# A hybrid decoder block on one core: the causal 31-tap convolution as three half-length filters on even and odd tokens

## The chip, the core and the metric

The kernel runs on one core of a Trainium2 chip. Its engines work at the same time, each on its own queue in order: TensorE (PE, with its weight loads PEld), VectorE (DVE), ScalarE (ACT), GpSimd (POOL) and SyncE (SP), which issues the transfers. The metric is the device time of one execution in microseconds, the median of several runs.

## The reference

2048 tokens of width 1024, in float32. A normalised input is projected by one matrix `w_in` into all sections; a convolution branch and an attention branch are gated, projected and merged.

```python
h = rmsnorm(x, norm_g)
glu_in, conv_gate, q, k, v, attn_gate, merge_logits = jnp.split(h @ w_in, SPLIT_POINTS, -1)
a, b = jnp.split(glu_in, 2, axis=-1)
c = a * jax.nn.sigmoid(b)                      # (2048, 1024)
c = conv(c, w_dw, causal, 31 taps, each channel by itself) + b_dw
c = silu(layernorm(c, ln_g, ln_b))
y_conv = (c * silu(conv_gate)) @ w_conv_out
a = sliding_window_attention(rope(q), rope(k), v, sinks)   # window 128, 16 heads, 4 KV heads
y_attn = (a * silu(attn_gate)) @ w_attn_out
g_conv, g_attn = jnp.split(jax.nn.sigmoid(merge_logits), 2, -1)
out = rmsnorm(x + (g_conv * y_conv + g_attn * y_attn) @ w_out, final_norm_g)
```

## The kernel before

The tokens are done in two sweeps `s` of T = 1024. Channels lie on the 128 partitions (eight groups `c` or `e` of 128), tokens along a row. Every float32 matrix product is made of three matmuls of 128x128 by 128x512, with operands split into a high and a low part: ScalarE makes the high part (`whi`, `hl`, `pt`), the low part is a subtraction in `split_lo` (L242), on GpSimd for weights (`wlo`) and on VectorE for activations. In sweep 0 the low parts of the weights of `w_in` and of the two branch outputs are computed and stored, in sweep 1 loaded.

A sweep goes through these stages. First the normalised input is transposed (`build_h_first`, `tpf`). Then come the projections (`project`): k, v and q with rope, and among them at eight places (`GLU_AFTER`) the two GLU halves of one channel group, `gb` (its sigmoid by ScalarE, `ev_b`, L415, into the row `glu`) and `ga` (multiplied into it by VectorE, `ev_a`, L419). Then the gates `ag`, `cg`, `ma` and `mc`, stored in DRAM, with the attention of 32 units beside them: scores `sc`, softmax in `ss` and `st`, transposes `tpp`, their split `pt`, the product `ov`, which ScalarE and VectorE add (L617, L618), and a split of the result. Then the attention's output projection `ya`, the convolution's `yc`, and `w_out` (`o`).

The convolution is VectorE's. `glu` holds 30 tokens of the sweep before (`glu_halo`, copied by GpSimd) and 1024 new ones. `conv_ops` gives 31 steps for a group: one multiplication with the bias (L389), then 30 multiply-adds (L393) on all 1024 tokens, each reading the row one token further on and adding to `cv` in place. After the last tap GpSimd adds `cv` to `csum`, and once all eight groups are done the layer norm follows (`ln_chain`, `ln_center`, `ln_chain2`, `ln_apply`). Then `u_op` multiplies it with the stored gate (`gated`, L711) and splits the product into `uT`, the operand of `yc`.

What sets the order: TensorE runs in the order in which the program is written. The class `Line` writes it: it counts planned microseconds of matmuls (`spend`) and hands out one background step, here a tap, whenever `every` of them have passed: `ROPE_EVERY` in the stage of k, v and q, `CONV_EVERY` beside the attention, `LN_EVERY` in the layer norm. The other engines' instructions are put in order by a scheduler, where evacuations of a psum buffer go with a higher priority. A tap that reads the result of the tap before waits for its end by a semaphore.

## Time and profile before

| | us |
|---|---|
| median of 3 runs | 2090.49 (2089.47 to 2090.71) |
| the profiled execution | 2090.34 |
| its span in the trace | 2088.4 |

| engine | busy us of the span |
|---|---|
| TensorE, matmuls | 2044.0 |
| VectorE | 1391.3 |
| ScalarE | 1032.4 |
| GpSimd | 483.2 |

Sweep 0 begins with the span, and the projections of sweep 1 at 1073.05 us. An instruction's duration holds its own start-up; on VectorE an instruction that does not wait for the one before it begins shortly before that one ends, so that durations add up to a little more than the time that they occupy.

### The profile page before, as it was taken

How to read it: one execution, taken by the hardware profiler on the slowest of the kernel's cores; microseconds unless marked ns; L12 is line 12 of the kernel's file. 1: busy time of each engine (PE TensorE's matmuls, PEld its weight loads, DVE VectorE, ACT ScalarE, POOL GpSimd, SP SyncE). 2: the span in 40 equal slices, each digit the busy share in tenths (PEclk: the TensorE clock that was granted, in tenths of full speed). 3: DMA queues.
4: the chain of work that ended last, by engine and by line, in shares of the span. 5: the costliest groups of instructions: out<-in, count | busy, mean ns of one | idle time of the engine just before them, and what ended most of it. 6: DMA issues, size and time to landing. Idle time of an engine off the chain costs nothing.

```text
span 2088.4 us, 27452 instructions
## 1 busy us (share of the span) xinstructions
PE 2044.0 (98%) x9256; PEld 1671.7 (80%) x9256; DVE 1391.3 (67%) x1901; ACT 1032.4 (49%) x2265; POOL 483.2 (23%) x336
## 2 busy tenths in 40 slices
PE   7999999998999999999999999999999999999998
PEld 6787888886777888888888888888888888888887
DVE  4979779998988348123559596698888934341324
ACT  6221377666667646112442214766777774621222
POOL 2445433433334222243001131121111110000200
PEclk9999999999999999999999999999999999999999
DMA  7344555554455775646344456555555578574432
GB/s 250 133 144 157 178 166 157 158 163 146 148 152 182 254 238 184 202 142 221 101 151 132 141 161 204 172 158 175 175 163 164 175 225 259 162 236 146 140 119 81
DMA packets 265820, 355.90 MB, mean 170 GB/s; under 512 B 28112, under 2 KB 126544, under 8 KB 265680
## 3 DMA queue, kind: packets, MB, share of 16 engines
q1 hardware_dynamic: 265680, 354.16, 53.3%
q8 instruction: 73, 1.20, 0.2%
q14 instruction: 67, 0.55, 0.1%
HBM read 234.51 MB, written 119.54 MB: 170 GB/s over the span
## 4 chain that ended last, share of the span: by engine, by line
PE 70%; DVE 4%; issue 2%; ACT 1%; DMA 0%; POOL 0%; SPq 0%; DVEq 0%; POOLq 0%; ACTq 0%
PE o L877 9%; PE mm_mc L281 8%; PE mm_yc L281 8%; PE mm_ya L281 8%; PE mm_ma L281 7%; PE mm_ga L281 5%; PE mm_cg L281 5%; PE mm_ag L281 4%; PE mm_gb L281 4%; DVE cv L393 2%; PE mm_q_a L281 2%; PE mm_q_b L281 2%; PE ov L614 2%; PE sc L566 2%; PE mm_v L281 1%
## 5 line engine op out<-in xcount | busy, mean ns | idle before, releaser
L393 DVE SCALAR_TENSOR_TENSOR cv<-glu,par,cv 128x1024 f32<-128x1024 f32 x480 | 675.9, 1408 | 6.7
L605 POOL TENSOR_SCALAR_AFFINE_SELECT pc<-pt 128x1024 fp32r<-128x1024 f32 x60 | 102.7, 1711 | 452.9 <-DVE pt L242 419.6
L877 PE MATMUL o<-wo,mT 128*128 128x512 f32 x768 | 181.3, 394 | 0.0
L877 PEld LDWEIGHTS o<-wo,mT 128*128 128x128 f32 x768 | 143.1, 188 | 32.1
L281 PE MATMUL mm_cg<-hT,whi_cg 128*128 128x512 f32 x512 | 163.2, 400 | 4.6 <-ACT glu L415 3.0
L281 PE MATMUL mm_ma<-hT,whi_ma 128*128 128x512 f32 x512 | 162.9, 399 | 4.0 <-ACT whi_ma L253 4.0
L281 PE MATMUL mm_ga<-hT,whi_ga 128*128 128x512 f32 x512 | 161.0, 395 | 0.2 <-ACT whi_ga L253 0.2
L281 PE MATMUL mm_ag<-hT,whi_ag 128*128 128x512 f32 x512 | 160.9, 395 | 0.0
L281 PE MATMUL mm_gb<-hT,whi_gb 128*128 128x512 f32 x512 | 160.6, 395 | 0.0
L281 PE MATMUL mm_mc<-hT,whi_mc 128*128 128x512 f32 x512 | 159.6, 393 | 0.0
L281 PE MATMUL mm_yc<-uT,whi_yc 128*128 128x512 f32 x512 | 159.4, 392 | 0.0
L281 PE MATMUL mm_ya<-aT,whi_ya 128*128 128x512 f32 x512 | 158.7, 391 | 0.0
L281 PEld LDWEIGHTS mm_cg<-hT,whi_cg 128*128 128x128 f32 x512 | 95.3, 191 | 25.2 <-ACT glu L415 3.4
L281 PEld LDWEIGHTS mm_ma<-hT,whi_ma 128*128 128x128 f32 x512 | 95.1, 190 | 23.9 <-ACT whi_ma L253 4.4
L281 PEld LDWEIGHTS mm_yc<-uT,whi_yc 128*128 128x128 f32 x512 | 96.2, 188 | 21.9
L281 PEld LDWEIGHTS mm_mc<-hT,whi_mc 128*128 128x128 f32 x512 | 96.0, 188 | 21.8
L281 PEld LDWEIGHTS mm_ya<-aT,whi_ya 128*128 128x128 f32 x512 | 96.1, 188 | 20.9
L281 PEld LDWEIGHTS mm_ga<-hT,whi_ga 128*128 128x128 f32 x512 | 94.5, 188 | 20.8 <-ACT whi_ga L253 1.0
L281 PEld LDWEIGHTS mm_gb<-hT,whi_gb 128*128 128x128 f32 x512 | 94.7, 188 | 20.0
L281 PEld LDWEIGHTS mm_ag<-hT,whi_ag 128*128 128x128 f32 x512 | 94.2, 188 | 19.7 <-ACT whi_ag L253 0.3
L584 ACT ACTIVATE ss<-ss,st 128x128 f32<-128x128 f32 x256 | 99.9, 391 | 19.2 <-DVE st L579 18.6
L815 POOL TENSOR_TENSOR lmc<-lmc,mp 128x512 f32<-128x512 f32 x32 | 41.9, 1309 | 275.5 <-DVE lmc L814 267.1
(363 smaller groups left out, 4356.4 us busy)
## 6 DMA issues: line engine op xcount, KB each, us to landing
qk<-d_q SPq DMA_DIRECT2D x256, 64.0 KB, 2.7
d_a<-ss SPq DMA_DIRECT2D x128, 128.0 KB, 1.9
aT<-d_a SPq DMA_DIRECT2D x32, 512.0 KB, 6.1
qk<-d_k SPq DMA_DIRECT2D x240, 64.0 KB, 2.1
raw_gb<-in_w_in_dram SPq DMA_DIRECT2D x34, 256.0 KB, 4.0
raw_ga<-in_w_in_dram SPq DMA_DIRECT2D x34, 256.0 KB, 3.4
raw_ag<-in_w_in_dram SPq DMA_DIRECT2D x32, 256.0 KB, 3.8
d_ag<-ag SPq DMA_DIRECT2D x32, 256.0 KB, 2.1
```

Of the source, the lines that this page charges most:

```text
L281: pe.matmul(out=ps, lhsT=a, rhs=b, start=(k == 0 and i == 0), stop=(k == KC - 1 and i == 2))
L393: dve.scalar_tensor_tensor(out=cv[c], in0=glu[c][:, j:j + T], scalar=tap(c, j), in1=cv[c], op0=ALU.mult, op1=ALU.add)
L566: pe.matmul(out=o, lhsT=q[:, h, :], rhs=r, start=(j == 0), stop=(j == 1))
L584: act.activation(out=sb[:, h, :], in_=sb[:, h, :], func=AF.Exp, scale=SCALE, bias=ngm[:, h:h + 1], accum_out=den[:, h:h + 1])
L605: pool.affine_select(out=pc, in_=f(pt), pattern=[[0, 2], [0, GQ], [1, P]], compare_op=ALU.is_ge, fill=0.0, base=0, channel_multiplier=-1)
L614: pe.matmul(out=ov, lhsT=vv, rhs=pp[:, i % 2], start=(i == 0), stop=(i == nm - 1))
L815: pool.tensor_tensor(out=g, in0=g, in1=mp[e][:, half * TH:(half + 1) * TH], op=ALU.add)
L877: pe.matmul(out=ps, lhsT=a[:, c0:c0 + P], rhs=r, start=(k == 0 and i == 0), stop=(k == KC - 1 and i == 2))
```

## The change

The convolution is written with three filters of 16, 15 and 16 taps on rows of half length. With the row split into even places e and odd places o, weights w0, w2, .. (16) and w1, w3, .. (15), and ts = w0+w1, w2+w3, .., the two halves of the result come from A = (even weights on o), B = (odd weights on e, 513 long) and S = (ts on e+o): one half is A + B shifted by one, the other S - A - B. For that

- `glu` and `cv` hold the tokens by parity: even places in the first half of the row, odd ones in the second (`NG` = 527 apart in `glu`, 512 in `cv`). The sigmoid, the GLU product and the halo copies write in this order, token by token in turn into the two halves; the layer norm works on it as it is, and `u_op` reads `cv` back in token order.
- a group has 50 steps in place of 31: 16 of A, 15 of B (into a new tile `fir`), the addition e+o, 16 of S (starting from -A), and two that join them and add the bias. 47 of the 50 are SCALAR_TENSOR_TENSOR, two TENSOR_SCALAR (the first taps of A and B), one an addition, on 512, 513 or 527 elements instead of 1024.
- `tsum` is made once at the start by two small VectorE instructions.
- `ROPE_EVERY` goes from 3.2 to 1.98 and `CONV_EVERY` from 2.4 to 1.49.

```diff
+NG = (HALO + T) // 2
...
-ROPE_EVERY = 3.2
-CONV_EVERY = 2.4
+ROPE_EVERY = 1.98
+CONV_EVERY = 1.49
...
+    NE = (TAPS + 1) // 2
+    tsum = const.tile([P, KC, NE], F32, name="tsum")
+    dve.tensor_copy(out=tsum, in_=par[:, :, 0:TAPS:2])
+    dve.tensor_tensor(out=tsum[:, :, 0:NE - 1], in0=tsum[:, :, 0:NE - 1], in1=par[:, :, 1:TAPS:2], op=ALU.add)
...
-            def first():
-                cv[c] = slot(C[c], [P, T], F32, f"cv{s}_{c}")
-                dve.tensor_scalar(out=cv[c], in0=glu[c][:, 0:T], scalar1=tap(c, 0), scalar2=cbias(c),
-                                  op0=ALU.mult, op1=ALU.add)
-
-            def nxt(j):
-                dve.scalar_tensor_tensor(out=cv[c], in0=glu[c][:, j:j + T], scalar=tap(c, j),
-                                         in1=cv[c], op0=ALU.mult, op1=ALU.add)
-                if j == TAPS - 1:
+            ge, go = (glu[c][:, i * NG:(i + 1) * NG] for i in range(2))
+            at = {}
+
+            def mac(out_, src, w, init):
+                if init is None:
+                    dve.tensor_scalar(out=out_, in0=src, scalar1=w, scalar2=None, op0=ALU.mult)
+                else:
+                    dve.scalar_tensor_tensor(out=out_, in0=src, scalar=w, in1=init[0], op0=ALU.mult,
+                                             op1=init[1])
+
+            def odd_tap(j):
+                if j == 0:
+                    cv[c] = slot(C[c], [P, T], F32, f"cv{s}_{c}")
+                    at["s"], at["a"] = cv[c][:, 0:TH], cv[c][:, TH:T]
+                    at["b"] = work.tile([P, TH + 1], F32, tag="fir", name=f"fir{s}_{c}", bufs=1)
+                mac(at["a"], go[:, j:j + TH], tap(c, 2 * j), (at["a"], ALU.add) if j else None)
+
+            def even_tap(j):
+                mac(at["b"], ge[:, j:j + TH + 1], tap(c, 2 * j + 1), (at["b"], ALU.add) if j else None)
+
+            def both():
+                dve.tensor_tensor(out=ge, in0=ge, in1=go, op=ALU.add)
+
+            def sum_tap(j):
+                mac(at["s"], ge[:, j:j + TH], tsum[:, c, j:j + 1],
+                    (at["s"], ALU.add) if j else (at["a"], ALU.subtract))
+
+            def join(i):
+                if i == 0:
+                    dve.scalar_tensor_tensor(out=at["a"], in0=at["a"], scalar=cbias(c), in1=at["b"][:, 1:],
+                                             op0=ALU.add, op1=ALU.add)
+                else:
+                    dve.scalar_tensor_tensor(out=at["s"], in0=at["s"], scalar=cbias(c),
+                                             in1=at["b"][:, 0:TH], op0=ALU.add, op1=ALU.subtract)
+                if i == 1:
...
+            ops += [lambda j=j: odd_tap(j) for j in range(NE)]
+            ops += [lambda j=j: even_tap(j) for j in range(NE - 1)]
+            ops.append(both)
+            ops += [lambda j=j: sum_tap(j) for j in range(NE)]
+            ops += [lambda i=i: join(i) for i in range(2)]
...
+        def by_parity(ap):
+            return ap.rearrange("p (o m) -> p m o", o=2)
+
+        def glu_of(c, half):
+            m0 = HALO // 2 + half * (TH // 2)
+            return by_parity(glu[c])[:, m0:m0 + TH // 2]
...
-                act.activation(out=glu[c][:, o:o + TH], in_=ps, func=AF.Sigmoid)
+                act.activation(out=glu_of(c, half), in_=ps.rearrange("p (m o) -> p m o", o=2),
+                               func=AF.Sigmoid)
...
-                g = glu[c][:, HALO + half * TH:HALO + (half + 1) * TH]
-                dve.tensor_tensor(out=g, in0=ps, in1=g, op=ALU.mult)
+                g = glu_of(c, half)
+                dve.tensor_tensor(out=g, in0=ps.rearrange("p (m o) -> p m o", o=2), in1=g, op=ALU.mult)
...
-            gated(uT[h][e], "cg", e, h, lambda: cv[e][:, h * TH:(h + 1) * TH])
+            g = load_gate("cg", e, h)
+            g2 = g.rearrange("p (m o) -> p m o", o=2)
+            m0 = h * (TH // 2)
+            dve.tensor_tensor(out=g2, in0=g2, in1=by_parity(cv[e])[:, m0:m0 + TH // 2], op=ALU.mult)
+            put_split(uT[h][e], g, dve)
```

The order of VectorE's queue, at the place where the taps of the last group begin in sweep 0, beside the attention (`cv_7` the taps' sums, `pt_2_7` a split of the attention's probabilities, `ss_2_6` the addition and the rest of a finished unit, `st_3_1` softmax statistics). Before:

```order
L389 TENSOR_SCALAR cv_7_5754<-glu_7_5041,par 128x1024
L393 SCALAR_TENSOR_TENSOR cv_7_5754<-glu_7_5041,par,cv_7_5754 128x1024 x3
L242 TENSOR_TENSOR pt_2_7_5297<-tpp_2_7_5291,pt_2_7_5297 128x512
L393 SCALAR_TENSOR_TENSOR cv_7_5754<-glu_7_5041,par,cv_7_5754 128x1024 x2
L618 TENSOR_TENSOR ss_2_6_4938<-ov_2_6_5320,ss_2_6_4938 64x256
L393 SCALAR_TENSOR_TENSOR cv_7_5754<-glu_7_5041,par,cv_7_5754 128x1024
L618 TENSOR_TENSOR ss_2_6_4938<-ov_2_6_5320,ss_2_6_4938 64x256
L574 COPY_PREDICATED ss_3_1_5355<-causal,sc_3_1_5346 128x512
L619 TENSOR_TENSOR ss_2_6_4938<-ss_2_6_4938 128x256
L578 TENSOR_REDUCE st_3_1_5358<-ss_3_1_5355 128x4
L242 TENSOR_TENSOR ss_2_6_4938<-ss_2_6_4938 128x256
L579 SCALAR_TENSOR_TENSOR st_3_1_5358<-st_3_1_5358,nsink 128x4
```

The same place after the change (a few lines of the file further down: L403 the multiply-adds, L248 `split_lo`, L664 and L665 the unit's end):

```order
L403 SCALAR_TENSOR_TENSOR cv_7_5933<-glu_7_5165,par,cv_7_5933 128x512
L403 SCALAR_TENSOR_TENSOR fir_7_5934<-glu_7_5165,par,fir_7_5934 128x513
L403 SCALAR_TENSOR_TENSOR cv_7_5933<-glu_7_5165,par,cv_7_5933 128x512
L403 SCALAR_TENSOR_TENSOR fir_7_5934<-glu_7_5165,par,fir_7_5934 128x513
L403 SCALAR_TENSOR_TENSOR cv_7_5933<-glu_7_5165,par,cv_7_5933 128x512
L403 SCALAR_TENSOR_TENSOR fir_7_5934<-glu_7_5165,par,fir_7_5934 128x513
L248 TENSOR_TENSOR pt_2_7_5428<-tpp_2_7_5422,pt_2_7_5428 128x512
L403 SCALAR_TENSOR_TENSOR cv_7_5933<-glu_7_5165,par,cv_7_5933 128x512
L403 SCALAR_TENSOR_TENSOR fir_7_5934<-glu_7_5165,par,fir_7_5934 128x513
L403 SCALAR_TENSOR_TENSOR cv_7_5933<-glu_7_5165,par,cv_7_5933 128x512
L403 SCALAR_TENSOR_TENSOR fir_7_5934<-glu_7_5165,par,fir_7_5934 128x513
L664 TENSOR_TENSOR ss_2_6_5059<-ov_2_6_5452,ss_2_6_5059 64x256
```

Where three taps of 1024 stood between the first tap and the split of `pt_2_7`, stand three of each of the two half filters (with their first taps ahead, unshown), taken in turn; the attention's instructions keep their order and their place among the planned steps.

At the start of VectorE's queue (`ssf` and `xf` the scaling of the first four input tiles, `nsink` the attention's sinks). Before:

```order
L354 TENSOR_SCALAR xf_2_84<-xf_2_84,ssf_157 128x1024
L134 TENSOR_SCALAR nsink<-sink_bc 128x16
L353 RECIPROCAL ssf_157<-ssf_157 128x1
L354 TENSOR_SCALAR xf_3_86<-xf_3_86,ssf_157 128x1024
L364 SCALAR_TENSOR_TENSOR hT_0_0_124<-tpf_0_178,par,hT_0_0_124 128x512
```

After:

```order
L360 TENSOR_SCALAR xf_2_84<-xf_2_84,ssf_160 128x1024
L135 TENSOR_SCALAR nsink<-sink_bc 128x16
L156 COPY tsum<-par 128x128
L157 TENSOR_TENSOR tsum<-tsum,par 128x8x15
L359 RECIPROCAL ssf_160<-ssf_160 128x1
L360 TENSOR_SCALAR xf_3_86<-xf_3_86,ssf_160 128x1024
L370 SCALAR_TENSOR_TENSOR hT_0_0_127<-tpf_0_181,par,hT_0_0_127 128x512
```

The two instructions that make `tsum` stand in front of the scaling of the fourth input tile.

## Rows read from the trace of the kernel before

**Rows 1.** page, part 1: busy us of each engine (share of the span), instructions

```profile
PE 2044.0 (98%) x9256; PEld 1671.7 (80%) x9256; DVE 1391.3 (67%) x1901; ACT 1032.4 (49%) x2265; POOL 483.2 (23%) x336
```

**Rows 2.** busy us by stretches: stretch, length, engines (instructions), mean granted clock, DMA

```profile
88.00:140.00 52.00, 49.89 (x222) 40.53 (x221) 39.59 (x54) 17.55 (x41) 21.93 (x17) 1.00 0.39 126
140.00:205.00 65.00, 60.31 (x255) 48.54 (x254) 63.95 (x51) 10.38 (x18) 31.03 (x20) 0.97 0.44 138
...
300.00:350.00 50.00, 48.68 (x235) 39.97 (x234) 42.04 (x59) 37.35 (x87) 17.80 (x13) 1.00 0.48 142
350.00:460.00 110.00, 109.41 (x519) 90.32 (x518) 101.00 (x135) 71.77 (x175) 42.43 (x28) 1.00 0.55 170
460.00:520.00 60.00, 52.96 (x244) 41.81 (x243) 55.29 (x68) 42.97 (x96) 18.41 (x12) 1.00 0.47 144
520.00:605.00 85.00, 79.78 (x360) 64.38 (x359) 73.99 (x101) 56.59 (x136) 33.17 (x22) 0.96 0.49 147
605.00:660.00 55.00, 50.90 (x231) 41.32 (x230) 54.35 (x66) 37.28 (x83) 17.54 (x12) 0.94 0.54 168
...
1073.05:2081.70 1008.65, 1008.60 (x4576) 828.25 (x4575) 643.09 (x894) 491.46 (x1066) 126.59 (x83) 1.00 0.54 169
```

**Rows 3.** VectorE, then ScalarE in order of time, 600 to 640 us

```profile
606.73 3.92 DVE L393 SCALAR_TENSOR_TENSOR cv<-glu,par,cv 128x1024 f32<-128x1024 f32 x3
...
611.17 3.31 DVE L393 SCALAR_TENSOR_TENSOR cv<-glu,par,cv 128x1024 f32<-128x1024 f32 x2
614.40 0.41 DVE L618 TENSOR_TENSOR ss<-ov,ss 64x256 f32<-64x256 f32 x1
...
614.84 0.36 ACT L617 COPY ss<-ov 64x256 f32<-64x256 f32 x1 [6.02 <-DVE ss L618]
```

**Rows 4.** waits of TensorE, 600 to 650 us: engine, line, releaser, us, times, longest

```profile
PE mm_ma L281 <- ACT whi_ma L253: 4.0, 1, 4.0
```

**Rows 5.** the taps: their group on the page; by tile, ns min/median/max

```profile
L393 DVE SCALAR_TENSOR_TENSOR cv<-glu,par,cv 128x1024 f32<-128x1024 f32 x480 | 675.9, 1408 | 6.7
...
L393 DVE SCALAR_TENSOR_TENSOR cv<-glu,par,cv x480: 1253/1285/2392, 54.0 to 1670.9; 128x1024 f32<-128x1024 f32 x160
...
L389 DVE TENSOR_SCALAR cv<-glu,par x16: 801/814/1610, 52.4 to 1618.7; 128x1024 f32<-128x1024 f32 x16
```

**Rows 6.** VectorE in order of time, 359 to 368 us: start, us (xcount merged)

```profile
359.31 1.28 DVE L393 SCALAR_TENSOR_TENSOR cv<-glu,par,cv 128x1024 f32<-128x1024 f32 x1
360.50 0.15 DVE L581 TENSOR_TENSOR st<-sink_bc,st 128x4 f32<-128x4 f32 x1
360.62 6.57 DVE L393 SCALAR_TENSOR_TENSOR cv<-glu,par,cv 128x1024 f32<-128x1024 f32 x5
```

**Rows 7.** two-operand 512-wide rows: VectorE's timeline at 17 us, VectorE's groups

```profile
17.30 1.41 DVE L364 SCALAR_TENSOR_TENSOR hT<-tpf,par,hT 128x512 fp32r<-128x512 f32 x2 [0.86 <-ACT hT L363]
...
L858 DVE SCALAR_TENSOR_TENSOR y<-y,yrs,gb 128x512 f32<-128x512 f32 x2 | 1.4, 749 | 0.0
```

**Rows 8.** other forms: VectorE's groups (busy, mean ns), and the line L711

```profile
L419 DVE TENSOR_TENSOR glu<-mm_ga,glu 128x512 f32<-128x512 f32 x32 | 21.9, 685 | 75.6 <-PE mm_ga L281 75.5
...
L676 DVE RECIPROCAL rstd<-rstd 128x256 f32<-128x256 f32 x8 | 13.2, 1709 | 32.5 <-ACT rstd L700 32.5
...
L322 DVE TENSOR_SCALAR x<-x,rs 128x512 f32<-128x512 f32 x16 | 7.0, 483 | 0.2
...
L711 DVE TENSOR_TENSOR lcg<-lcg,cv x32: 677/688/695, 802.3 to 1846.9; 128x512 f32<-128x512 f32 x32
```

**Rows 9.** the chain of waits in order of time: start, us, what

```profile
1904.37 88.57 PE mm_yc L281 x384
```

**Rows 10.** start: issue of par, its landing (median us), VectorE behind

```profile
3.15 0.48 SPq L136 DMA_DIRECT2D par<-in_par_dram  x1
...
par<-in_par_dram SPq DMA_DIRECT2D x1, 140.0 KB, 7.3
...
10.76 0.16 DVE L353 RECIPROCAL ssf<-ssf 128x1 f32<-128x1 f32 x1 [0.33 <-ACT ssf L351]
```

More of the change, by code (lines that the diff above doesn't have):

```diff
@@ L402, in nxt @@
                         line.start(ln_chain())
-            ops.append(first)
-            for j in range(1, TAPS):
-                ops.append(lambda j=j: nxt(j))
-            return ops
+            ops += [lambda j=j: odd_tap(j) for j in range(NE)]
[3 more added lines that the diff above has]
+            ops += [lambda i=i: join(i) for i in range(2)]
+            return ops
+        def by_parity(ap):
[3 more added lines that the diff above has]
+            return by_parity(glu[c])[:, m0:m0 + TH // 2]
         def glu_items(c):
@@ L412, in ev_b @@
                     glu[c] = slot(glu_slot[c], [P, HALO + T], F32, f"glu{s}_{c}")
-                    pool.tensor_copy(out=glu[c][:, 0:HALO], in_=glu_halo[:, c, :])
-                o = HALO + half * TH
-                act.activation(out=glu[c][:, o:o + TH], in_=ps, func=AF.Sigmoid)
+                    pool.tensor_copy(out=by_parity(glu[c])[:, 0:HALO // 2], in_=glu_halo[:, c, :].rearrange(
+                        "p (m o) -> p m o", o=2))
+                act.activation(out=glu_of(c, half), in_=ps.rearrange("p (m o) -> p m o", o=2),
+                               func=AF.Sigmoid)
             def ev_a(half, ps):
-                g = glu[c][:, HALO + half * TH:HALO + (half + 1) * TH]
-                dve.tensor_tensor(out=g, in0=ps, in1=g, op=ALU.mult)
+                g = glu_of(c, half)
+                dve.tensor_tensor(out=g, in0=ps.rearrange("p (m o) -> p m o", o=2), in1=g, op=ALU.mult)
                 if half == 1:
                     if s + 1 < NSWEEP:
-                        pool.tensor_copy(out=glu_halo[:, c, :], in_=glu[c][:, T:T + HALO])
+                        pool.tensor_copy(out=glu_halo[:, c, :].rearrange("p (m o) -> p m o", o=2),
+                                         in_=by_parity(glu[c])[:, TH:NG])
                     line.bg.extend(conv_ops(c))
@@ L707, in sweep @@
         aT, uT = [[None] * KC, [None] * KC], []
-        def gated(dst, kind, e, half, other):
-            g = load_gate(kind, e, half)
-            dve.tensor_tensor(out=g, in0=g, in1=other(), op=ALU.mult)
-            put_split(dst, g, dve)
         def a_op(e, h):
```

## The prediction

> **What bounds the kernel now.** I read the page's first part, then the busy time by stretches, then what TensorE waited for, then single instructions. TensorE is busy for 2044.0 of 2088.4 us and VectorE for 1391.3 [rows 1], so the time is TensorE's, and a faster VectorE is worth only what TensorE waits for it. The stretches [rows 2] show where that is. From its first projection to its last matmul sweep 1 takes 1008.65 us and TensorE is busy in 1008.60 of them: nothing is to be had there. All the idle time lies in sweep 0 between 88 and 660 us: 52.00-49.89 = 2.11, then 4.69, 1.32, 0.59, 7.04, 5.22 and 4.10 us, 25.1 in all. In three of these stretches the mean granted clock is also below 1 (0.97, 0.96, 0.94: part of the stretch at the lower of the two levels, after a wait), worth 0.03x65 + 0.04x85 + 0.06x55 = 8.7 us. So 34 us is the most that this change can return.
>
> VectorE is the reason for most of it: it is busy for 63.95 of the 65.00 us from 140, 55.29 of the 60.00 from 460 and 54.35 of the 55.00 from 605 [rows 2]. How this reaches TensorE is seen at 606 us [rows 3]: VectorE runs three taps of the convolution, then two more, and only then, at 614.40, the attention's addition. ScalarE, which takes its queue in order, stands for 6.02 us before the copy that needs this addition, with weight casts (whi_ma) behind that copy; TensorE's longest wait of this stretch, 4.0 us, is for whi_ma [rows 4].
>
> **The taps.** Before: 16 times (two sweeps, eight channels) one TENSOR_SCALAR and 30 SCALAR_TENSOR_TENSOR over 1024 tokens. One lasts 1285 ns as a rule; the mean is 1408 [rows 5], the rest being overlap with GpSimd, 480x0.123 = 59 us. What a tap occupies depends on its follower [rows 6]: an independent one starts 360.50-359.31 = 1.19 us after it, a tap that reads its result later: five take 6.57, 1.31 each. In VectorE's order 199 of 496 taps stand right behind the one that they read. So they occupy 199x1.31 + 297x1.19 - 16x0.47 (the TENSOR_SCALAR is shorter, 0.81 as a rule) = 606 us.
>
> After: 800 instructions on half rows: 752 SCALAR_TENSOR_TENSOR, 32 TENSOR_SCALAR, 16 additions. Over 512 the first lasts 749 ns, and two independent ones take 1.41, so one starts 0.66 after the other [rows 7]; with the dependency's 0.12 it is 0.78. TENSOR_SCALAR is 483 instead of 749 ns [rows 8]. The odd and the even filter alternate in the new order, which leaves 205 of 800 right behind the one that they read: 205x0.78 + 595x0.66 - 32x0.27 = 544 us. The multiplications fall by a quarter, but the fixed part, 2x749-1285 = 213 ns an instruction, eats most of that. The saving is 62 us, 31 a sweep; the overlap with GpSimd, whose work is the same, I leave at 59.
>
> The pace stays: 50 steps at 1.49 are 74.5 of the planner's microseconds for a channel, 31 at 2.4 were 74.4; 50x1.98 = 99.0 against 31x3.2 = 99.2. So a channel is handed out over the same TensorE work, and the 31 us spread evenly over the 610 us from 50 to 660: 5.1% of each stretch.
>
> **What the even-odd layout costs.** The GLU product (VectorE) and the sigmoid (ScalarE) now write element by element in turn into two regions 527 elements apart, and the product reads one operand so. No row shows such steps. Below, nothing is added: the product costs 685 ns from PSUM, the gate product 688 from SBUF [rows 8], so the source does not matter; a gain is excluded, since no two-operand row of this size is under 0.67. Above stands the slowest row per element, the reciprocal, 1709 ns for 256 [rows 8]: 3.42 for 512, 2.73 more. I take one more pass over the elements, 1285-749 = 0.54, which lies near the lower row. That is 16x0.54 = 8.6 us of VectorE a sweep, and the saving shrinks to 22.4 us, 3.7% of each stretch.
>
> [...]
>
> The sigmoids may grow by as much, 16 a sweep on a ScalarE that is busy for 37.28 of 55.00 us in the last stretch [rows 2]: room enough, but up to 0.5 us later for a psum buffer. The gate product reads in the new order too, 8.6 us a sweep at the same price: hidden, since the last one starts at 1846.9 and mm_yc, which reads its result, at 1904.37 [rows 8, 9]. Were that cover gone, each microsecond would delay TensorE by one.
>
> **Small things.** The two tsum instructions stand in front of the last input tile's scaling. They read par, issued at 3.15 and landed 7.3 us later, at 10.45; the reciprocal behind them ran at 10.76 after 0.33 us of idling [rows 10]. Each is under the 0.48 of a 512-wide TENSOR_SCALAR: between 0 and 2x0.48-0.33 = 0.63 us later; I take 0.3, fully on TensorE's path, as TensorE waits for that tile. The layer norm's sums stand a few matmuls later in TensorE's order, GpSimd's halo copies, running sums and weight splits swap neighbours, and the transfers are the same in number: nothing, as GpSimd is busy for less than half of each stretch [rows 2].
>
> **The sum.** A stretch returns its share of VectorE time, at most its idle time: at 3.7%, 1.9 + 2.4 + 1.3 + 0.6 + 2.2 + 3.1 + 2.0 = 13.5 us in the order of the stretches. The three clock losses shrink with the idle time of their stretches, by 2.4/4.69, 3.1/5.22 and 2.0/4.10: 1.0 + 2.0 + 1.6 = 4.6. With tsum: 13.5 + 4.6 - 0.3 = 17.8. The profiled execution took 2090.34, 1.94 outside its span and 0.15 below the median of the runs, 2090.49; so about **2072.5 us**. Late next is ScalarE's queue, whose table loads and softmax steps the taps don't touch.
>
> **The rivals.** *The layout is free.* For it: equal prices whatever the source [rows 8]. Against: nothing in the trace steps like that. All 5.1% count: 2.1 + 3.3 + 1.3 + 0.6 + 3.1 + 4.3 + 2.8 = 17.5, clock 1.4 + 2.8 + 2.2 = 6.4, tsum -0.3: 2066.7. If the 5 us that 350-460 does not need also shorten 460-520, where 3.9 us would be left, 2063.
>
> *The stalls stay.* TensorE's last wait names ScalarE [rows 4], and ScalarE stands in front of the attention's chain in a fixed order. If the new order only puts other steps last, each stretch keeps its stall: 2090.6. Against it: the 6.02 us of ScalarE end in VectorE's addition, behind five taps [rows 3].
>
> *The layout is dear, and the kernel slower.* One mechanism: each GLU product blocks VectorE, with the next taps and attention steps behind it. It decides from 31/16 = 1.9 us more per product, 2.6 in all; at the reciprocal's price VectorE has 16x2.73-31 = 12.7 us more a sweep, 2.1% of each stretch: over the 477 us of the seven stretches 9.9 more idle, clock 8.7x9.9/25.1 = 3.4, tsum 0.3: 2103.9. For it: operand and result both step. Against: every product in the trace but the reciprocal runs at one rate.
>
> **How the numbers follow.** Forecast 0.46, free layout 0.27, stalls stay 0.12, dear layout 0.15. A measurement of this kernel tells 0.2%, 4.2 us. Faster takes the first two and a fifth of the third (a part of the stalls going): 0.75; same the rest of the third and a bit of the dear case near its turning point: 0.11; slower 0.14. The range reaches from 2060, under the free layout, to 2091, where the stalls stay; it leaves out the dear case and some of the far end of the free one.
>
> **What would show it.** Right: tap instructions near 0.75 us and about 650 us in all, with the overlaps, where there were 692 [rows 5]; the GLU product near 1.2 us; TensorE's idle time of 88 to 660 us about halved, sweep 1 still without any. A product at 0.69 means the free layout; one above 2.6 the dear one. Wrong: taps saving their 31 us a sweep while the idle time stays, or a new idle stretch behind GpSimd's halo copies.

## The result and the profile after

The changed kernel takes 2095.72 us (median of 10 runs, 2094.49 to 2096.66), the kernel before 2090.88 us on the same chip: a ratio of 1.0023 [1.0013, 1.0033], slower by 4.8 us where 18 us faster was forecast. The profiled execution has a span of 2093.0 us.

The page's first part of the kernel after, against [rows 1]: TensorE's work is the same, VectorE has 59.1 us less, ScalarE 17.5 more.

```profile
PE 2044.1 (98%) x9256; PEld 1667.8 (80%) x9256; DVE 1332.2 (64%) x2207; ACT 1049.9 (50%) x2269; POOL 446.0 (21%) x336
```

The three large groups of taps on the page, against the first of [rows 5]:

```profile
L403 DVE SCALAR_TENSOR_TENSOR cv<-glu,tsum,cv 128x512 f32<-128x512 f32 x256 | 210.2, 821 | 5.0
L403 DVE SCALAR_TENSOR_TENSOR cv<-glu,par,cv 128x512 f32<-128x512 f32 x240 | 199.3, 830 | 0.2
L403 DVE SCALAR_TENSOR_TENSOR fir<-glu,par,fir 128x513 f32<-128x513 f32 x224 | 187.9, 839 | 1.0
```

By line and tile (ns min/median/max), the median tap, the GLU product, its sigmoid and the gate product, against [rows 5, 8]:

```profile
L403 DVE SCALAR_TENSOR_TENSOR cv<-glu,tsum,cv x256: 727/752/1847, 90.7 to 1672.9; 128x512 f32<-128x512 f32 x128
...
L464 DVE TENSOR_TENSOR glu<-mm_ga,glu x32: 1065/1094/1135, 34.0 to 1623.5; 128x512 f32<-128x512 f32 x32
...
L459 ACT ACTIVATE glu<-mm_gb x32: 1050/1082/1111, 25.9 to 1616.6; 128x512 f32<-128x512 f32 x32
...
L765 DVE TENSOR_TENSOR lcg<-lcg,cv x32: 703/714/723, 805.1 to 1854.4; 128x512 f32<-128x512 f32 x32
```

With the small groups of a filter's first taps, the addition and the two joins (57.9 us) the taps have 655.3 us; 650 was forecast. The product that writes element by element in turn into two regions takes 1.09 instead of 0.69 us, the sigmoid 1.08 instead of 0.60; the gate product, which only reads so (from halves of 2048 bytes), 0.71 instead of 0.69.

Busy time by stretches, against [rows 2] (the same stretches of sweep 0; the last is sweep 1):

```profile
88.00:140.00 52.00, 48.13 (x207) 38.95 (x206) 34.08 (x59) 17.81 (x40) 18.86 (x16) 0.97 0.38 122
140.00:205.00 65.00, 60.85 (x257) 48.48 (x256) 61.62 (x70) 9.90 (x18) 27.08 (x19) 0.98 0.41 129
300.00:350.00 50.00, 50.00 (x243) 41.57 (x242) 41.99 (x72) 34.06 (x78) 15.90 (x12) 1.00 0.48 145
350.00:460.00 110.00, 104.41 (x485) 85.18 (x485) 89.47 (x154) 75.62 (x182) 33.52 (x26) 0.98 0.53 161
460.00:520.00 60.00, 55.70 (x257) 43.68 (x255) 58.58 (x93) 36.31 (x81) 18.44 (x15) 1.00 0.45 136
520.00:605.00 85.00, 78.29 (x358) 61.84 (x358) 66.27 (x112) 62.18 (x141) 27.48 (x21) 1.00 0.50 156
605.00:660.00 55.00, 51.74 (x244) 41.85 (x244) 52.21 (x88) 31.84 (x77) 15.18 (x12) 1.00 0.51 157
1075.90:2086.30 1010.40, 1009.29 (x4577) 828.27 (x4575) 613.21 (x1045) 508.90 (x1074) 111.87 (x84) 1.00 0.54 169
```

VectorE is busy for less in six of the seven stretches, and TensorE's idle time is not less: 27.9 us in them where there were 25.1. It has only moved, above all out of 460 to 520 us (7.04 to 4.30) and into 350 to 460 (0.59 to 5.59). What the granted clock takes, reckoned as the prediction did, is less than before: 0.03x52 + 0.02x65 + 0.02x110 = 5.1 us for 8.7. Over all of 50 to 660 us, before and after:

```profile
50.00:660.00 610.00, 584.39 (x2659) 475.38 (x2658) 537.54 (x640) 330.92 (x751) 243.66 (x161) 0.99 0.50 156
```

```profile
50.00:660.00 610.00, 582.12 (x2647) 470.58 (x2646) 505.62 (x785) 323.62 (x730) 215.74 (x159) 0.99 0.49 153
```

VectorE's work falls by 31.9 us there, and so, in a stretch of fixed length, its own idle time rises from 72.5 to 104.4. What it idles for (waits of VectorE in this stretch: line, releaser, us, times, longest), before and after:

```profile
DVE glu L419 <- PE mm_ga L281: 23.9, 5, 9.3
DVE st L586 <- ACT ss L584: 15.5, 9, 4.8
DVE pt L242 <- ACT pt L599: 14.3, 5, 3.8
```

```profile
DVE glu L464 <- PE mm_ga L287: 33.0, 5, 9.3
DVE st L632 <- ACT ss L630: 23.6, 9, 5.6
DVE pt L248 <- ACT pt L645: 22.8, 8, 4.3
```

Most of the saved time is spent waiting for ScalarE's softmax and splits (16.6 us more in the last two rows) and for TensorE itself (9.1 more). Fixed stretches cut the program at other places in each kernel, so the rest goes by stages: the time from TensorE's first matmul of one kind to the first of the next (`q to ag` is from the first of q to the first of `ag`, and so on). A stage holds the same matmuls in each of these kernels, in the same order but for a few around the layer norm's sums. In us, for the kernel before, and as differences from it:

| kernel | q to ag | to cg | to ma | to mc | to ya | sweep 1, gb to ya |
|---|---|---|---|---|---|---|
| before | 143.29 | 158.66 | 202.54 | 112.63 | 93.55 | 743.65 |
| after | +2.62 | +2.46 | +0.10 | -2.59 | +0.26 | +1.61 |
| e1 layout only | +0.53 | +2.23 | +1.91 | -0.71 | +0.01 | 0 |
| e2 dense GLU | +2.60 | +1.02 | -3.19 | -1.63 | +0.20 | +0.01 |
| e4 narrow taps | -5.73 | -0.62 | -14.62 | -2.25 | +0.07 | +0.01 |
| e5 before, 902 tokens | +2.27 | -2.66 | +0.65 | -8.06 | 0 | 0 |
| e6 read in steps | +2.68 | +1.02 | -2.86 | -3.04 | +0.07 | +0.01 |
| e9 before, pace -2% | +1.70 | 0 | -0.19 | +0.22 | +8.03 | +3.80 |
| e10 before, pace +2% | +1.69 | -0.01 | -0.02 | -0.17 | +0.02 | +0.41 |
| e11 e6, pace +2% | +2.65 | +1.09 | -2.95 | -6.16 | +0.58 | -0.05 |
| e12 e6, steps in pairs | +2.72 | +1.12 | -3.23 | -6.17 | +0.10 | +0.01 |
| e13 before, no tables | +0.12 | -2.71 | -4.41 | -2.93 | 0 | 0 |
| e14 e5, no tables | +2.15 | -2.70 | -11.16 | -6.01 | 0 | 0 |
| e15 after, no tables | +2.62 | -2.71 | -7.98 | -2.79 | +0.07 | +0.01 |

The first matmul of all (mm_gb at 18.52 us before) moves by between -0.8 and +0.3, with `tsum` and without; the stages that are not shown last the same within 0.1 us, but for `ya` in e9 to e11. The change loses 5.1 us in the first two stages, gains 2.5 in the next two, and loses 1.6 in sweep 1.

One stall makes the first stage's loss. TensorE's waits from 88 to 140 us, before and after:

```profile
PE tpv L499 <- ACT vs L519: 2.1, 1, 2.1
```

```profile
PE tpv L545 <- ACT vs L565: 3.9, 1, 3.9
```

ScalarE in order of time there (start, us, what, idle time before it), before and after:

```profile
92.21 0.40 ACT L513 CAST vd<-vd 128x256 fp32r<-128x256 f32 x1 [10.62 <-DVE vd L502]
...
93.29 0.59 ACT L519 COPY vs<-mm_v 128x512 f32<-128x512 f32 x1
```

```profile
93.44 0.41 ACT L559 CAST vd<-vd 128x256 fp32r<-128x256 f32 x1 [11.47 <-DVE vd L548]
...
94.96 0.37 ACT L559 CAST vt<-tpv 128x256 fp32r<-128x256 f32 x1 [0.35 <-DVE vt L248]
95.23 0.59 ACT L565 COPY vs<-mm_v 128x512 f32<-128x512 f32 x1
```

The copy `vs`, which TensorE needs, waits in ScalarE's queue behind work that needs VectorE: 1.2 us more for `vd`, to which VectorE comes later, and then behind a second cast `vt` that it used to precede. Behind the longer wait TensorE's granted clock is lower, too. Busy time from 96 to 100 us, the granted clock third from the end, before and after:

```profile
96.00:100.00 4.00, 4.00 (x19) 3.23 (x19) 4.00 (x9) 3.38 (x9) 1.57 (x1) 1.00 0.00 0
```

```profile
96.00:100.00 4.00, 4.00 (x14) 3.23 (x15) 3.96 (x10) 2.11 (x7) 0.00 (x0) 0.61 0.00 0
```

By single microseconds the clock after is 0.95, 0.50, 0.50 and 0.50. The stall grows by 1.8 us and about 4.00x0.39 = 1.6 us of work are lost at the lower clock; 0.8 of that come back by 237 us.

### The profile page after: what moved, and what is told of

Its sections match the earlier page's. It is cut to its first block, busy times and chain, and to the rows that moved or that the text cites. A ratio compares the mean times of both kernels' runs of the same rounds, so it can differ in the third digit from the quotient of the medians.

```text
span 2093.0 us, 27798 instructions
## 1 busy us (share of the span) xinstructions
PE 2044.1 (98%) x9256; PEld 1667.8 (80%) x9256; DVE 1332.2 (64%) x2207; ACT 1049.9 (50%) x2269; POOL 446.0 (21%) x336
## 4 chain that ended last, share of the span: by engine, by line
PE 73%; DVE 17%; ACT 5%; DMA 2%; issue 2%; SPq 1%; POOL 0%; DVEq 0%; ACTq 0%; POOLq 0%
PE o L922 8%; PE mm_mc L287 8%; PE mm_yc L287 8%; PE mm_ya L287 8%; DVE cv L403 6%; PE mm_gb L287 6%; PE mm_ga L287 5%; PE mm_cg L287 4%; PE mm_ag L287 4%; PE mm_ma L287 4%; PE mm_q_b L287 4%; DVE fir L403 4%; PE mm_q_a L287 4%; PE mm_v L287 2%; PE ov L660 1%
## 5 line engine op out<-in xcount | busy, mean ns | idle before, releaser
L403 DVE SCALAR_TENSOR_TENSOR cv<-glu,tsum,cv 128x512 f32<-128x512 f32 x256 | 210.2, 821 | 5.0
L403 DVE SCALAR_TENSOR_TENSOR cv<-glu,par,cv 128x512 f32<-128x512 f32 x240 | 199.3, 830 | 0.2
L403 DVE SCALAR_TENSOR_TENSOR fir<-glu,par,fir 128x513 f32<-128x513 f32 x224 | 187.9, 839 | 1.0
L651 POOL TENSOR_SCALAR_AFFINE_SELECT pc<-pt 128x1024 fp32r<-128x1024 f32 x60 | 79.8, 1329 | 413.8 <-DVE pt L248 413.8
```

Of the source, the lines that this page charges most:

```text
L403: dve.scalar_tensor_tensor(out=out_, in0=src, scalar=w, in1=init[0], op0=ALU.mult, op1=init[1])
L651: pool.affine_select(out=pc, in_=f(pt), pattern=[[0, 2], [0, GQ], [1, P]], compare_op=ALU.is_ge, fill=0.0, base=0, channel_multiplier=-1)
```

## The experiments

**e1_layout_only and e2_dense_glu: the layout's price, alone in the kernel before and taken out of the changed one.**

```diff
 # e1, from the kernel before: GLU, sigmoid and halo copies write in turn into two halves
...
-                act.activation(out=glu[c][:, o:o + TH], in_=ps, func=AF.Sigmoid)
+                act.activation(out=glu_of(c, half), in_=ps.rearrange("p (m o) -> p m o", o=2),
+                               func=AF.Sigmoid)
...
 # e2, from the changed kernel: the same two regions, each written in one piece
-            return by_parity(glu[c])[:, m0:m0 + TH // 2]
+            return glu[c].rearrange("p (o m) -> p o m", o=2)[:, :, m0:m0 + TH // 2]
...
```

> The kernel before with one thing of the change: sigmoid, GLU product and halo copies write token by token in turn into two regions 527 apart. The 31 taps stay, so the convolution mixes wrong tokens; every queue has the order of before. Theory L (the layout eats the gain): the 7 us of VectorE and 8 us of ScalarE a sweep that the dearer sigmoid and product take are put onto TensorE's waits, 2090.9 becomes 2100 or more. Theory Q (the waits are set by the fixed order of ScalarE's and GpSimd's queues, not by VectorE's total): under 4 us more, 2091 to 2095.

> The changed kernel with the same two regions in the GLU row, but each of them written as one contiguous run of 256, so that the convolution mixes wrong tokens; every queue keeps the order of the changed kernel. Sigmoid and product should be back at 0.60 and 0.69 us. Theory L: with the layout's price gone the saved taps show, 2095.7 becomes 2080 or less. Theory Q: 2090 to 2096, a few us at most.

e1: 2094.46 us against 2091.17, ratio 1.0017 [1.0008, 1.0026]. e2: 2089.6, 0.9991 [0.9982, 1.0000]. In e1 the product takes 1.10 and the sigmoid 1.09 us, in e2 they are back at 0.69 and 0.60. The layout costs 3.3 us in the kernel before and 6.1 (2095.7 - 2089.6) in the changed one. The times lie in theory Q's range for e1 and 0.4 us below it for e2; theory L is out. So the layout's cost is real, and not the whole miss: without it the new taps bring 1.6 us (the interval reaches from nothing to 3.8), though VectorE's busy time of the whole run is then 1321.8 us, 69.5 less than before.

**e3_halo_on_dve: does GpSimd's halo copy hold things up?** It waits for taps in the changed kernel (74.5 us in ten waits) and stands in front of weight splits.

```diff
-                    pool.tensor_copy(out=by_parity(glu[c])[:, 0:HALO // 2], in_=glu_halo[:, c, :].rearrange(
+                    dve.tensor_copy(out=by_parity(glu[c])[:, 0:HALO // 2], in_=glu_halo[:, c, :].rearrange(
```

> The changed kernel with the copy of the 30 old tokens into the GLU row made by VectorE in place of GpSimd. After the change GpSimd stands 74.5 us in 10 waits before this copy for the last taps of the row's former user, with weight splits and running sums queued behind it. If that is what took the gain back (theory P): GpSimd's waits for taps before this copy are gone, TensorE's waits for wlo_ga and wlo_gb (5.8 us) with them, 2088 to 2091. If those waits only take the place of others (theory Q): within 2 us of 2095.7.

2095.69 us, 1.0022 [1.0014, 1.0031]: the time does not move, as theory Q had it. The wait took another place: GpSimd now waits 78.7 us for the last taps in front of the running sum (`csum`), where it waited 19.9, and TensorE's waits for `wlo_ga` and `wlo_gb` stay (5.7 us for 5.8). So the copy is no cause by itself; a kernel in which GpSimd never waits for taps was not run.

**e4_narrow_taps: much less VectorE work in the same order.**

```diff
-                mac(at["a"], go[:, j:j + TH], tap(c, 2 * j), (at["a"], ALU.add) if j else None)
+                n = QN if j else TH        # QN = 256; the other two filters alike
+                mac(at["a"][:, 0:n], go[:, j:j + n], tap(c, 2 * j), (at["a"][:, 0:n], ALU.add) if j else None)
```

> The changed kernel with all taps but the first of each filter on 256 of the 512 or 513 columns, which leaves half of the convolution out: 44 instructions a channel group about 0.27 us shorter, some 95 us of VectorE a sweep. Theory V (what the prediction took: TensorE's waits shrink with VectorE's time): nearly all idle time of 50 to 660 us goes, 2060 to 2068. Theory Q: waits for ScalarE and GpSimd remain, 2075 to 2092.

2066.35 us, 0.9882 [0.9869, 0.9896]. Busy time from 50 to 660 us:

```profile
50.00:660.00 610.00, 599.71 (x2771) 492.82 (x2770) 412.79 (x815) 353.81 (x799) 215.67 (x169) 0.99 0.53 164
```

VectorE has 124.7 us less there than before, TensorE idles 10.3 us instead of 25.6. This lies in theory V's range: VectorE's time does count. But 125 us a sweep bring 24.8, 0.2 us for each, where the prediction's rule, which caps each stretch at its idle time, gives all of its 34.

**e5_before_902: the forecast saving alone, in the 31 old steps.**

```diff
-                dve.scalar_tensor_tensor(out=cv[c], in0=glu[c][:, j:j + T], scalar=tap(c, j),
-                                         in1=cv[c], op0=ALU.mult, op1=ALU.add)
+                dve.scalar_tensor_tensor(out=cv[c][:, 0:TN], in0=glu[c][:, j:j + TN], scalar=tap(c, j),
+                                         in1=cv[c][:, 0:TN], op0=ALU.mult, op1=ALU.add)   # TN = 902
```

> The kernel before with 30 of the 31 taps on 902 of 1024 tokens, which leaves an eighth of the convolution out: each is 0.127 us shorter, 31 us of VectorE a sweep, as much as the three filters save, in 31 steps at the old pace and with the old layout. Theory V (31 us of VectorE are worth 18 to 24, and the 50 steps in their new places give them back): 2067 to 2075. Theory R (the first 31 us are worth little wherever they are saved, since the waits hang on chains through ScalarE; e4's 125 us of VectorE less between 50 and 660 brought 25, 0.2 for one): 2084 to 2091.

2081.97 us against 2091.16, 0.9955 [0.9942, 0.9967]: 9.2 us, between the two theories.

```profile
50.00:660.00 610.00, 590.69 (x2696) 481.28 (x2695) 507.27 (x648) 326.03 (x755) 236.68 (x162) 0.99 0.51 157
```

VectorE's 507.27 us are the changed kernel's 505.62, with no steps in the layout and no short instructions. The prediction's own rule gives 24 us for this kernel (its free layout). The stages show where they stay away: 88 to 205 us, from which 2.1 + 3.3 + 1.4 = 6.8 were expected, lie in the q stage, which loses 2.3, most of it by the same stall (2.9 us there, with a lower clock behind it). `cg` to `ma`, from which over 10 were expected (460 to 605 us: 3.1 + 4.3 and 2.8 for the clock), loses 0.7. `ag` to `cg` gives 2.7, and `ma` to `mc` 8.1, more than was hoped for. There the 4.0 us wait of [rows 4] and the lost clock around it are gone:

```profile
605.00:660.00 55.00, 55.00 (x262) 45.58 (x262) 51.96 (x71) 34.86 (x83) 21.49 (x12) 1.00 0.56 173
```

So the chain that the prediction read at 606 us [rows 3] was VectorE's, and shorter taps dissolved it; the other stalls did not follow it.

**e6_strided_read: the row in token order, read in steps.**

```diff
-            ge, go = (glu[c][:, i * NG:(i + 1) * NG] for i in range(2))
+            ge, go = (glu[c].rearrange("p (m o) -> p o m", o=2)[:, i] for i in range(2))
...
-                act.activation(out=glu_of(c, half), in_=ps.rearrange("p (m o) -> p m o", o=2),
-                               func=AF.Sigmoid)
+                act.activation(out=glu_of(c, half), in_=ps, func=AF.Sigmoid)   # contiguous; product alike
```

> The changed kernel with the GLU row in token order: sigmoid and product write contiguously, the half filters read every second element, and the sum of even and odd tokens is written in place to every second element. Every queue keeps the order of the changed kernel; all of the computation is done. The gate product already reads such a pattern at 0.71 where 0.69 were contiguous. If only writing in steps is dear: taps stay near 0.75, sigmoid 0.60, product 0.69, and the time is that of e2, 2088 to 2091. If reading in steps is dear too: taps near 1.1, 2140 or more.

2089.69 us, 0.9993 [0.9984, 1.0002]: 6.0 us less than the changed kernel, all of the layout's cost. The product is back at its old duration, and a tap that reads every second element lasts as long as one that reads a row in one piece (a median of 752 ns in both). The addition e+o, which also writes every second element here, takes 0.71 us in both kernels, so of the steps in these kernels only the writing in turn into two regions is dear (1.09 us for the product):

```profile
L462 DVE TENSOR_TENSOR glu<-mm_ga,glu x32: 660/691/694, 33.7 to 1615.7; 128x512 f32<-128x512 f32 x32
...
L403 DVE SCALAR_TENSOR_TENSOR cv<-glu,tsum,cv x256: 728/752/1858, 90.5 to 1665.1; 128x512 f32<-128x512 f32 x128
```

**e7_two_steps and e8_pace_m: the places of the steps in the changed kernel.** e7 hands out two of the 50 steps at a time, e8 each one 2% earlier.

```diff
 # e7
-ROPE_EVERY = 1.98
-CONV_EVERY = 1.49
+ROPE_EVERY = 3.96
+CONV_EVERY = 2.98
...
-            return ops
+            return [lambda f=f, g=g: two(f, g) for f, g in zip(ops[0::2], ops[1::2])]
 # e8
-ROPE_EVERY = 1.98
-CONV_EVERY = 1.49
+ROPE_EVERY = 1.94
+CONV_EVERY = 1.46
```

> The changed kernel with its 50 steps a channel group handed out two at a time at twice the interval, as coarse as the taps before. If the fine steps lose time by standing in turn with the attention's instructions: 2080 to 2090. Theory R: the same work in nearly the same places, within 3 us of 2095.7.

> The changed kernel with the steps handed out 2% faster (1.94 and 1.46 in place of 1.98 and 1.49): no work changes, the scheduler puts some instructions elsewhere. If the order alone moves the waits by several us (theory O), the time differs from 2095.7 by 2 to 6, up or down; if the order does not matter at this size, by under 1.5.

e7: 2092.85 us, 1.0010 [1.0001, 1.0019], 2.9 less than the changed kernel, at the edge of theory R's 3. e8: 2101.38, 1.0050 [1.0038, 1.0063], 5.7 more, as theory O had it. The instructions are as long as before (the means of the three large groups of taps are 821, 832 and 845 ns in e7 and 821, 827 and 845 in e8, where they were 821, 830 and 839); the order is worth as much as the layout.

**e9_before_pace_m and e10_before_pace_p: the same in the kernel before.**

```diff
-ROPE_EVERY = 3.2
-CONV_EVERY = 2.4
+ROPE_EVERY = 3.13     # e10: 3.27
+CONV_EVERY = 2.35     # e10: 2.45
```

> The kernel before with a tap handed out a little earlier: ROPE_EVERY 3.13 instead of 3.2, CONV_EVERY 2.35 instead of 2.4 (2% less; the taps, their number and the layout as before). Nothing takes more or less time; only the places of the steps among the matmuls move. Theory O (a place of the steps moves the time by some us, and the places of the kernel before are good ones): slower by 2 to 8 us, ratio 1.001 to 1.004, with sweep 1 starting later than 1072.9 us. Theory F (the 50 steps of a group cost the change what it lacks, whatever the places): ratio 0.9995 to 1.0005.

> The kernel before with a tap handed out a little later: ROPE_EVERY 3.27, CONV_EVERY 2.45 (2% more). Theory O: slower by 2 to 8 us, ratio 1.001 to 1.004. Theory F: ratio 0.9995 to 1.0005.

e9: 2108.85 us against 2090.8, 1.0086 [1.0072, 1.0100]. e10: 2129.03, 1.0184 [1.0168, 1.0199]. Both far above what either theory gave, and not for the reason it gave: from `ag` to `mc` the stages stay within 0.2 us, as the order there hardly changes. e9 loses 8.0 from `mc` to `ya`, 3.9 in `ya` and 3.8 in sweep 1, e10 22.7 in `ya` (110.71 us instead of 87.99) and 13.7 in that of sweep 1. TensorE's longest wait in e10:

```profile
PE mm_ya L281 <- DVE mp L791: 31.0, 2, 19.7
```

`mp` is the evacuation (the product that empties the psum buffer) of a block of `ya`, in front of which the program writes out in one lump (`line.finish`) what is left of the layer norm and of `uT`, if that block's part of `uT` isn't written. The layer norm's first subtraction runs at 743.6 us before, at 757.8 in e10, which leaves much to that lump, and at 732.3 in e9, beside more of the gates `mc`: there TensorE waits 2.3 us for ScalarE's `mc` and 3.2 for weights of `ya`, and never between 700 and 900 us before. The old pace lies in a gap between the two, and the changed kernel, at 747.8, kept it; e8, at 733.5, lost 5.4 from `mc` to `ya`.

**e11_strided_read_pace_p and e12_strided_read_two_steps: e6 with other places.**

```diff
 # e11, from e6
-ROPE_EVERY = 1.98
-CONV_EVERY = 1.49
+ROPE_EVERY = 2.02
+CONV_EVERY = 1.52
 # e12, from e6: the pairs and paces of e7
```

> The changed kernel with its row in token order, the half filters reading every second element (as in the run before of this form, 0.9993), and now ROPE_EVERY 2.02 and CONV_EVERY 1.52 instead of 1.98 and 1.49 (2% more). Theory O: the time moves by 2 to 8 us against that run, either way; if the places of the steps were chance in it, as likely down as up: 2082 to 2097. Theory F: within 1 us of that run, ratio 0.999 to 1.0.

> Row in token order, half filters reading every second element, and the 50 steps handed out two at a time (25 of them, ROPE_EVERY 3.96, CONV_EVERY 2.98). The first alone brought 6 us against the changed kernel, the second 3. Theory F (the small steps cost): both add up, about 2087, ratio 0.998, the first kernel here that is faster than the one before with its output right. Theory O: the places of the paired steps brought their 3 us by chance in another layout; anywhere from 2083 to 2094, ratio 0.996 to 1.001.

e11: 2120.49 us, 1.0140 [1.0126, 1.0154], outside both theories' ranges, over the same edge (28.2 us of waits for `mp`). e12: 2084.24 us against 2090.8, 0.9968 [0.9955, 0.9980]: 6.6 us faster than the kernel before and 11.5 than the changed one: theory O's range, and more than the sum that theory F gives.

```profile
50.00:660.00 610.00, 588.50 (x2685) 477.90 (x2684) 508.50 (x797) 325.42 (x752) 220.41 (x162) 0.99 0.51 156
```

VectorE's work is that of e6 (506.12 us); TensorE idles 21.5 us instead of 23.8. Both kernels gain the same 3.1 us more than e6 in `ma` to `mc` (-6.2 against -3.0), one with 50 single steps, the other with 25 pairs: so in this stage it is the place of the steps, not their number.

**e13_before_no_tables, e14_before_902_no_tables and e15_after_no_tables: how much is ScalarE's?** In e13 ScalarE takes the exponential that the softmax uses in place of sigmoid and silu, e14 adds e5's edit to that, and e15 makes e13's edit in the changed kernel. ScalarE's table loads in the kernel before, from 50 to 660 us:

```profile
L434 ACT ACT_TABLE_LOAD x27 | 34.6, 1283 | 0.5
L584 ACT ACT_TABLE_LOAD x26 | 33.4, 1283 | 0.5
L415 ACT ACT_TABLE_LOAD x8 | 10.3, 1283 | 0.1
L582 ACT ACT_TABLE_LOAD x6 | 7.7, 1283 | 0.1
```

Of these 67 loads 64 stand at a change between the exponential and sigmoid or silu, three at one from silu to sigmoid; the 125 times that one of the three follows itself there is none, and copies and casts between them have none either.

```diff
-                act.activation(out=glu[c][:, o:o + TH], in_=ps, func=AF.Sigmoid)
+                act.activation(out=glu[c][:, o:o + TH], in_=ps, func=AF.Exp, scale=0.01)
...
-                act.activation(out=g, in_=ps, func=func)      # Silu, Sigmoid
+                act.activation(out=g, in_=ps, func=func, scale=0.01)      # Exp
```

> The kernel before with the gates' and the GLU's sigmoid and silu replaced by an exponential with the scale 0.01, the function that the softmax beside them uses: the output is not the reference's. A table load of 1.283 us stands on ScalarE at every change of function; between 50 and 660 us there are 67 of them, 86 us of ScalarE's 331, and nearly all of them go. VectorE's work is as before (537 us there); the order moves by itself in places. Theory S (TensorE's stalls are chains through ScalarE's queue as much as VectorE's, which is why VectorE's saved time came back as waits on ScalarE): TensorE's idle time between 50 and 660 us falls from 25.6 to under 18, ratio 0.996 or less. Theory V (VectorE's busy share alone sets them): idle 23 or more, ratio 0.998 to 1.001.

> Both together in the kernel before: taps on 902 tokens (31 us of VectorE less in a sweep, the time that the change saves there) and no changes of function on ScalarE beside the attention; the output is not the reference's. Taps on 902 alone brought 9 us. Theory S: more than either alone, idle between 50 and 660 us under 13, and the taps are worth as much as alone or more (against the run with all 1024 tokens and no table loads: 8 to 20 us). Theory V: as the taps alone, ratio 0.994 to 0.997.

> The changed kernel, layout and half filters as they are, with the same exponential in place of the gates' and the GLU's functions; the output is not the reference's. Theory S: idle between 50 and 660 us from 27.9 to under 18, and faster than the kernel before without table loads by some us, since ScalarE no longer eats VectorE's saving. Theory V: idle 25 or more, ratio 1.0 to 1.003.

Against 2090.16 us: e13 2081.22, 0.9957 [0.9940, 0.9974]; e14 2070.92, 0.9906 [0.9891, 0.9921]; e15 2079.4, 0.9951 [0.9936, 0.9966]. Busy time from 50 to 660 us in e13, e14 and e15:

```profile
50.00:660.00 610.00, 589.75 (x2708) 482.50 (x2707) 544.11 (x648) 241.46 (x690) 252.27 (x163) 0.99 0.50 157
```

```profile
50.00:660.00 610.00, 596.43 (x2745) 489.12 (x2744) 516.34 (x660) 250.34 (x720) 244.72 (x165) 0.99 0.52 161
```

```profile
50.00:660.00 610.00, 589.30 (x2712) 481.91 (x2711) 518.01 (x802) 250.19 (x703) 227.79 (x163) 0.99 0.51 158
```

ScalarE's busy time there falls from 330.9 to 241.5 in e13, VectorE's over the whole run stays (1390.8 for 1391.3), the other ScalarE instructions last as before (the gates' 0.59 for 0.60), and 8.9 us are gained: theory V falls, by this ratio. Theory S, as put, holds only half: the idle time falls to 20.2 us, not under 18. Taps on 902 tokens bring 10.3 us more (e14 against e13) where they brought 9.2 with the table loads, and TensorE idles 13.6 us, just above theory S's 13. In total the gains add, but not stage by stage. `ag` to `cg` gives 2.7 to each saving alone and 2.7 to both; `ma` to `mc` gives 8.1 to the taps, 2.9 to the table loads and 6.0 to both; `cg` to `ma`, where the taps alone lose 0.7 and the table loads alone bring 4.4, gives 11.2 to both. So some stalls go with either saving, and some only with both. The changed kernel without table loads is not told from e13 (1.8 us faster, the intervals overlap), where with them it is 4.8 slower than the kernel before. So ScalarE had eaten part of its saving, but its idle time, 20.7 us, is again above theory S's 18: a third thing comes up. TensorE's longest waits in e15, from 50 to 660 us:

```profile
PE sc L612 <- DVE ss L620: 11.9, 8, 2.9
PE tpv L545 <- ACT vs L565: 3.9, 1, 3.9
PE mm_q_b L287 <- DVE rb_q__1_1554 L513: 3.4, 1, 3.4
```

In the kernel before no wait of the scores `sc` is among the seven longest of this stretch; the other two are the old ones, one unmoved and one grown.

## Why the prediction was wrong

**What bounds the kernel** was right: TensorE's time does not change, and nearly all of the idle time that a faster VectorE can touch lies in sweep 0. Sweep 1 was to be without any; it now waits once for a low weight part to be loaded (0.6) and once for `whi_ma` (0.5), and loses 1.6 us in all; without the layout (e2, e6) it does not.

**The taps** were right, a little low: 655 us of durations for the 650 forecast, and in e2, where they stand alone, 34.8 us of VectorE less a sweep where 31 were forecast. The 59 us for GpSimd's overlap held: in the kernel before the 338 multiply-adds beside which GpSimd is idle last 1289 ns at most, and all that last longer, up to 2392, run beside one of its instructions; after the change the means of the three groups stand above their medians by 59 us again.

**The layout** was right in kind: 0.41 us more a product and 0.48 more a sigmoid, with 0.54 taken for each. Between its forecast and the free layout the prediction put 5.8 us; e2 and e6 measure 6.1 and 6.0. That they agree is luck: the 5.8 came from the share of VectorE's time that failed, 1.6 of the 6 us lie in sweep 1, where nothing was forecast, and in the kernel before the same layout costs 3.3 (e1). One part was off: the price is the writing's. A product that writes in turn into the two regions goes from 0.69 to 1.09 us, but the gate product, which only reads so, from 0.69 to 0.71: 0.03 and not the 0.54 taken; it is hidden as forecast. Reading every second element, in e6, costs nothing (the taps' median is 752 ns in both).

**`tsum`**: 0.3 us forecast; the first matmul starts 0.23 us later. That is no more than the scatter: in e2 and e6, which make `tsum` too, it starts 0.02 and 0.03 earlier, in e10, which does not, 0.25 later.

**The sum failed**, at one step: "A stretch returns its share of VectorE time, at most its idle time." By it 31 us a sweep were worth 24 us. Measured by themselves (e5) they are worth 9.2, 0.3 for each; with no table loads beside them 10.3; 125 us are worth 24.8. The rule takes a busy VectorE for a queue that empties evenly, and one stall, the 4.0 us of [rows 4], for the pattern of all. Its own sign of being wrong came: the taps save their 31 us a sweep and TensorE's idle time stays, 27.9 us for 25.1. What the traces show is a chain through two engines with fixed orders: VectorE finishes its taps earlier and then waits for ScalarE, whose copies and casts stand behind others that wait for VectorE: from 50 to 660 us its work falls by 31.9 us, and its waits for ScalarE's softmax and splits grow by 16.6. At the stall that was read, time came back (`ma` to `mc`, 8.1 in e5); where the wait hangs on the place of one copy in ScalarE's queue (the q stage), shorter taps changed the places and the stall grew.

**The clock term** (4.6 us back) came out near its size, 8.7 - 5.1 = 3.6 us in the profiled executions, but by luck: it was to follow the idle time of its stretches. From 520 to 605 us the idle time grew (5.22 to 6.71) and the lost clock went (0.96 to 1.00); in the stretches from 88 and from 350 us, where none was lost, it fell to 0.97 and 0.98.

**What was left out**: that the places of the steps have a price of their own, a term that the prediction put at nothing. "So a channel is handed out over the same TensorE work" is true of the pace, and it kept the kernel off the edges on both sides of it, which 2% would have reached (18 and 38 us in e9 and e10). Within the pace the 50 steps fall between other instructions than the 31 did. In the changed kernel's own order without the layout, 1.6 us of the 9.2 arrive (e2); with the row read in steps and pairs of steps 6.6 (e12).

So the 4.8 us, put together step by step: -9.2 for VectorE's time (e5), +7.6 for the new steps in their places (e2 against e5), +6.1 for the layout (e2), 4.5 in all. Another order of the steps would share it out otherwise, as e1's 3.3 us for the layout show. Of the rivals, *the stalls stay* (2090.6 us) came nearest; it had 0.12, because the row for it, TensorE's wait for ScalarE, was read as VectorE's doing further up [rows 3, 4]. For that stall e5 bears this out; for the others it was both engines', and e13 shows ScalarE's part. The *dear layout* is excluded by the product's 1.09 us.

The 7.6 us are a difference of two kernels and not one stall that was followed through; by stages it is 6.4 in `ma` to `mc` and 3.7 in `ag` to `cg`, less 3.8 in `cg` to `ma`. That it is the places and not the number of steps is shown for 3.1 us of `ma` to `mc` (e11, e12) and open for the rest.

## What to carry to other kernels

Where the bound engine waits for chains that cross two in-order queues, do not turn a saving on one of them into time by its share: look at each stall for the instruction that comes last and what stands in front of it in its own queue, and do not count on more than a run shows: here it was a third of VectorE's saving (e5). Before and after such a change, move the hand-out pace by 2% either way: here that alone moved the time by up to 38 us, more than everything the change did. To split a row into even and odd elements, try writing it in one piece and reading it in steps: here the product took 0.69 us so and 1.09 when it wrote in turn, and the taps' median stayed at 0.75.

## What the runs showed of the hardware

- Writing 512 float32 alternately into two regions 2108 bytes apart costs VectorE 0.41 us (0.685 to 1.094) and ScalarE 0.48 (0.600 to 1.082); reading from two regions 2048 bytes apart costs VectorE 0.03 (0.688 to 0.714), reading every second element nothing (743 and 752 ns median in both kernels), nor does writing every second element in place (e+o, 709 ns in both).
- A wait of 2.1 us at 94 us left TensorE's granted clock at 1.00 from 96 to 100 us; waits of 2.9 (e5) and 3.9 us at the same place were followed by 0.72 and 0.61 there, after the longest at 0.50 for three of the four microseconds. So there a wait of 1.8 us more cost nearly twice that. The length alone does not tell: in the kernel before a wait of 1.96 us that ended at 553.8 us was followed by 0.50 from 554 to 557.
- Taking 67 table loads of 1.28 us off ScalarE in the stretch from 50 to 660 us, with its other instructions kept, brought 8.9 us: about 0.1 for each microsecond, less than VectorE's 0.3, though ScalarE is the engine waited for in 12.2 of the 25.6 us that TensorE idles there before, VectorE in 6.2.
